# Max-unpooling on one core: the first image made in eight VectorE instructions on half images instead of four on whole ones

## The chip, the cores and the metric

The kernel runs on one core of one Trainium2 chip. The metric is the device time of one execution in microseconds (us), and the tables give the median of several executions. "Span" is the time from the first to the last instruction in the profiled execution. It is about 1.3 us shorter than the device time of the same execution (71.54 us against a span of 70.2 us before the change).

## The reference

Each input element goes to one of four places in its own 2x2 output block. The other three places get zero.

```python
batch, channels, h, w = 16, 64, 32, 32          # x float32, indices 0..3, kernel_size 2
output = np.zeros((batch, channels, 2 * h, 2 * w), dtype=np.float32)
# for every b, c, i, j:
idx = indices[b, c, i, j]
output[b, c, 2 * i + idx // 2, 2 * j + idx % 2] = x[b, c, i, j]
```

The indices arrive as 64-bit integers, so 4.19 MB of x and 8.39 MB of indices are read and 16.78 MB are written.

## The kernel before

The 1024 images (batch times channels) lie on 128 partitions, T = 8 images on each. They are made in four groups of G = 2. All loads are issued before anything else, from one queue, in the order: indices of image 0, indices of images 1 and 2, all of x, the other indices. VectorE waits for all of x and then makes each image with four instructions, one for each place in the 2x2 block: (index == place) * x, written with stride 2.

```python
nc.vector.wait_ge(x_in, 16).then_inc(x_in, -16)          # all of x
for t in range(T):
    g, k = t // G, t % G
    if t in (0, FIRST):                                  # FIRST = 3
        ...                                              # wait for the indices' first or second part
    if k == 1 and t != FIRST and g:
        continue                                         # image already made together with its neighbour
    n = 1 if k == 1 or t + 1 == FIRST or not g else 2    # images in one instruction
    if g == NG - 1:
        nc.vector.wait_ge(stored_0, 16).then_inc(stored_0, -16)   # group 3 reuses group 0's buffer
    ...
    for pidx in range(4):
        op = nc.vector.scalar_tensor_tensor(
            out=o_c[:, k : k + n, :, pidx // 2, :, pidx % 2],
            in0=idx_c[:, t : t + n], scalar=pidx, in1=x_c[:, t : t + n],
            op0=mybir.AluOpType.is_equal, op1=mybir.AluOpType.mult)
    if k + n == G:
        op.then_inc(made, 1)                             # group complete

for g in range(NG):                                      # the queue that also issued the loads
    nc.sync.wait_ge(made, g + 1)
    nc.sync.dma_start(out=out_v[g], in_=out_t[g]).then_inc(stored if g else stored_0, 16)
```

## Time and profile before

| | before |
|---|---|
| device time, median of 3 (range) | 71.61 us (71.50 to 71.64) |
| span of the profiled execution | 70.2 us |
| VectorE (DVE in the profile) busy | 35.9 us, 24 instructions, 19.5 to 55.4 us |
| DMA engines, share of the span with a packet | 97.6% |
| first store: issued, first packet | 28.70 us, 30.64 us |

The transfers, as the page lists them (what is moved, issuing queue, count, KB each, median us from issue to landing; the two small loads of indices are left out):

```profile
out_dram<-out_t SPq DMA_DIRECT2D x4, 4096.0 KB, 13.5
idx_t<-in_indices_dram SPq DMA_DIRECT2D x1, 5120.0 KB, 30.1
x_t<-in_x_dram SPq DMA_DIRECT2D x1, 4096.0 KB, 18.4
```

The large load of indices takes 30.1 us to land because it stands last in the queue, behind the other loads, and not because it is slow: its own packets run only from 18.5 to 31.1 us. The other views of this profile are read in the prediction.

### The profile page before, as it was taken

To read this page: it belongs to the slowest core of one execution; us is meant where nothing else is said; L and a number is where in the kernel's file an instruction comes from. 1 tells how busy PE (TensorE), PEld (TensorE's weight loads), DVE (VectorE), ACT (ScalarE), POOL (GpSimd) and SP (SyncE) were. 2 spreads that over 40 slices of the span, in tenths; PEclk is the share of its full clock that TensorE was granted. 3 is DMA by queue.
4 is the path that set the end of the run, shared out by engine and by line. 5 is a ranking of instruction groups with operands and counts; after the bars stand their busy time and mean duration, and the time that the engine had idled before them with its cause. 6 is when DMAs were issued, how large, how long until landed. Compare 5 with 4: busy or idle time off the path is not lost.

```text
span 70.2 us, 77 instructions
## 1 busy us (share of the span) xinstructions
DVE 35.9 (51%) x24; POOL 0.2 (0%) x4
## 2 busy tenths in 40 slices
DVE  0000000000089999999999999999999500000000
POOL 1000000000000000000000000000000000000000
DMA  4999996969988899869799796969798896969790
GB/s 84 397 425 439 448 597 299 597 299 523 448 373 373 373 653 467 373 299 560 336 485 411 317 579 299 597 299 579 317 541 355 373 523 299 597 299 579 317 579 19
DMA packets 1152, 29.36 MB, mean 418 GB/s; under 512 B 128, under 2 KB 128, under 8 KB 128
## 3 DMA queue, kind: packets, MB, share of 16 engines
q1 hardware_dynamic: 1152, 29.36, 97.6%
HBM read 12.58 MB, written 16.78 MB: 418 GB/s over the span
## 4 chain that ended last, share of the span: by engine, by line
DVE 46%; DVEq 4%; issue 1%
DVE out_t L140 46%; DVEq L190 4%
## 5 line engine op out<-in xcount | busy, mean ns | idle before, releaser
L140 DVE SCALAR_TENSOR_TENSOR out_t<-idx_t,x_t 128x1024 f32<-128x1024 int32 (+1 forms) x24 | 35.9, 1572 | 19.5 <-DVEq L128 19.5
L176 POOL MEMSET const-bfloat16-1.0<- 128x1 bf16 x1 | 0.1, 101 | 0.0
L176 POOL MEMSET const-uint8-127<- 128x1 uint8 x1 | 0.1, 101 | 0.0
L176 POOL MEMSET const-float32-0.0<- 128x1 f32 x1 | 0.1, 98 | 0.2 <-issue 0.2
L176 POOL MEMSET const-float32-1.0<- 128x1 f32 x1 | 0.1, 98 | 0.0
## 6 DMA issues: line engine op xcount, KB each, us to landing
out_dram<-out_t SPq DMA_DIRECT2D x4, 4096.0 KB, 13.5
idx_t<-in_indices_dram SPq DMA_DIRECT2D x1, 5120.0 KB, 30.1
x_t<-in_x_dram SPq DMA_DIRECT2D x1, 4096.0 KB, 18.4
idx_t<-in_indices_dram SPq DMA_DIRECT2D x1, 2048.0 KB, 9.1
idx_t<-in_indices_dram SPq DMA_DIRECT2D x1, 1024.0 KB, 4.7
```

What stands on the lines that cost most here:

```text
L140: op = nc.vector.scalar_tensor_tensor(out=o_c[:, k : k + n, :, pidx // 2, :, pidx % 2], in0=idx_c[:, t : t + n], scalar=pidx, in1=x_c[:, t ...
L176: nc = _bacc.Bacc("TRN2", target_bir_lowering=False, num_devices=1)
L190: with _tile.TileContext(nc) as tc:
```

## The change

The apparent intent is to give VectorE smaller first pieces. Only image 0 is affected: its rows are cut in two, and the four instructions run once for each half. No load, wait or store moves.

```diff
-            for pidx in range(4):
-                op = nc.vector.scalar_tensor_tensor(
-                    out=o_c[:, k : k + n, :, pidx // 2, :, pidx % 2],
-                    in0=idx_c[:, t : t + n],
-                    scalar=pidx,
-                    in1=x_c[:, t : t + n],
+            parts = (slice(0, H // 2), slice(H // 2, H)) if t == 0 else (slice(0, H),)
+            for rows in parts:
+                for pidx in range(4):
+                    op = nc.vector.scalar_tensor_tensor(
+                        out=o_c[:, k : k + n, rows, pidx // 2, :, pidx % 2],
+                        in0=idx_c[:, t : t + n, rows],
+                        scalar=pidx,
+                        in1=x_c[:, t : t + n, rows],
...
```

More of the change, by code (lines that the diff above doesn't have):

```diff
@@ L138 @@
             )
-            for pidx in range(4):
-                op = nc.vector.scalar_tensor_tensor(
-                    out=o_c[:, k : k + n, :, pidx // 2, :, pidx % 2],
-                    in0=idx_c[:, t : t + n],
-                    scalar=pidx,
-                    in1=x_c[:, t : t + n],
-                    op0=mybir.AluOpType.is_equal,
-                    op1=mybir.AluOpType.mult,
-                )
+            parts = (slice(0, H // 2), slice(H // 2, H)) if t == 0 else (slice(0, H),)
[6 more added lines that the diff above has]
+                        in1=x_c[:, t : t + n, rows],
+                        op0=mybir.AluOpType.is_equal,
+                        op1=mybir.AluOpType.mult,
+                    )
             if k + n == G:
```

## The prediction

> **What bounds the kernel now.** I read the page's rows by engine and by slice first, then the DMA queue row, then the groups of instructions with shapes kept apart, the timeline around the stores, the queue's own waits, the busy time by stretches, and last the chain that ended last. The chain comes last because here it can mislead.
>
> The page: the slices of VectorE and of the DMA engines, and the queue row (packets, megabytes, share of the 16 engines' time).
>
> ```profile
> DVE  0000000000089999999999999999999500000000
> ...
> DMA  4999996969988899869799796969798896969790
> ...
> q1 hardware_dynamic: 1152, 29.36, 97.6%
> ```
>
> VectorE works only in the middle 36 us of the 70.2 us span. The DMA engines hold a packet for 97.6% of the span. The dips to 6 and 7 in the row are no pauses: a packet here lasts up to 1.5 us against a slice of 1.76 us, and a whole packet seems to be counted in the slice in which it starts. In longer stretches (columns: stretch, length, VectorE busy, GpSimd busy, clock, DMA share, GB/s) the share is level:
>
> ```profile
> 1.00:12.00 11.00, 0.00 (x0) 0.00 (x0) 1.00 1.04 429
> 12.00:30.00 18.00, 10.49 (x10) 0.00 (x0) 1.00 1.01 437
> 30.00:42.00 12.00, 12.00 (x9) 0.00 (x0) 1.00 1.01 434
> 42.00:55.40 13.40, 13.37 (x7) 0.00 (x0) 1.00 1.00 433
> ```
>
> Loads give way to stores around 31 us, and no stretch drops. From the trace's packet records I laid out every packet by start and duration: from 1.6 us on, 16 packets are in flight at every moment until 69.4 us. On each engine the first packet of the first store starts 6 ns after the last load's closing packet has begun; the first such start is at 30.64 us, the last at 31.11. A 32 KB packet takes 1.213 us, so 16 engines move 16 x 32768 B / 1.213 us = 432 GB/s, and 29.36 MB need 67.9 us. Add 1.0 us before the first packet, about 0.6 us of ragged start, and 0.4 us after the last packet, and the 70.2 us is accounted for. **The kernel is bound by bytes through the DMA engines**, and the only question about any VectorE change is whether a store comes to the queue too late.
>
> The groups, and where the stores are issued:
>
> ```profile
> L140 DVE SCALAR_TENSOR_TENSOR out_t<-idx_t,x_t 128x1024 f32<-128x1024 int32 x16 | 18.3, 1217 | 19.5 <-DVEq L128 19.5
> L140 DVE SCALAR_TENSOR_TENSOR out_t<-idx_t,x_t 128x2048 f32<-128x2048 int32 x8 | 17.7, 2282 | 0.0
> ...
> 19.50 35.87 DVE L140 SCALAR_TENSOR_TENSOR out_t<-idx_t,x_t 128x1024 f32<-128x1024 int32 x24 [19.50 <-DVEq L128]
> 28.70 27.03 SPq L153 DMA_DIRECT2D out_dram<-out_t  x4
> ```
>
> VectorE starts at 19.50 us, when x has landed, and then never idles (35.87 us busy of 35.87). The first store is issued at 28.70 us, once images 0 and 1 are done. Eight instructions lie between, so from start to start one on 1024 elements takes about (28.69 - 19.50) / 8 = 1.135 us with the overlap taken out, which the trace's start times confirm (1135 ns).
>
> The chain and the queue's own waits:
>
> ```profile
> 19.50 12.00 DVE out_t L140 x11
> ...
> 44.36 11.01 DVE out_t L140 x5
> ...
> SPq L153 <- DVE out_t L140: 51.9, 4, 26.3
> ```
>
> Both seem to say that VectorE holds the stores back. They only say that the sequencer that issues stores waits for VectorE. While it waits, the DMA engines still work through what was issued before. The chain ends with VectorE at 55.37 us; the remaining 15 us are transfers.
>
> [...]
>
> **The change part by part.** It *removes* four instructions on 1024 elements (image 0) and *adds* eight on 512. Elements, results and order of images are the same, and no wait moves: image 0 still starts only when both inputs are there, the one increment that releases the first store is still on the last instruction of image 1, and the loads and stores are the same descriptors. The built program confirms it: VectorE goes from 24 to 28 such instructions, and the queue's rows are unchanged.
> - Old image 0: 4 x 1135 = 4540 ns from start to start.
> - New image 0: [...]8 x 601 = 4808 ns. Their profiled duration should be about 1217 - 512 x (2282 - 1217)/1024 = 685 ns, so busy time as summed by the group rises more, unless overlap is merged.
> - Difference: four more fixed parts, 4 x 68 = **0.27 us** on VectorE. All later VectorE work shifts by it: the end from 55.37 to 55.64 us, store issues from 28.70 to 28.97 us for the first and from 55.4 to 55.7 us for the last.
>
> What lies on the path to the end? The first load needed 1.0 us from issue to first packet. With that, the first store could start at 28.97 + 1.0 = 29.97 us, while its engines are busy with loads until 30.64 us: 0.66 us of slack remain of 0.93. Later stores have more: the last is issued at 55.7 us and ready at 56.7, while store 2 occupies the engines until 59.7, 3 us of slack. The fourth group reuses the first group's buffer and waits for the first store, landed by 41.5 us; VectorE gets there only at 46.6, so that wait stays empty. Sum on the path: 0.27 us of extra work, 0 us of it seen. I expect 71.6 us, the time of before.
>
> **The rivals.** *One: the first store is late and VectorE's cost shows in full.* This holds if the latency of an issue under a loaded queue is not 1.0 us but near the 1.94 us seen between issue (28.70) and first packet (30.64). For it: the trace only bounds that latency from above for a busy queue. Against it: the 6 ns gap between last load and first store looks like a queue already full, not one just in time. It would make 71.6 + 0.27 = 71.9 us. *Two: a half image costs its whole duration instead of its start-to-start time.* Then 8 x 685 - 4540 = 0.94 us are added, the first store is ready at 30.64 us, just as the first engine comes free; the time is 71.6 to 71.7, and with both rivals together about 72.5 (+1.3%). Against it: start-to-start has been below duration for every neighbour in the trace. *Three: finer pieces speed something up*, by letting the first store go sooner. Against it: the store needs all of images 0 and 1, and no load is cut to match the halves. Even a VectorE of zero cost would find the engines busy with loads until 30.64. It would make 71.6, at best some hundredths less.
>
> **Range and chances.** The three times of before span 71.50 to 71.64. Below, nothing in the change removes a byte, so 71.4 covers scatter only. Above, 71.9 covers rival one in full. To pass 2% the time must move by 1.43 us, which no rival reaches: slower 0.01, faster 0.01, within 2% 0.98.
>
> **What would show it.** Right: a group of eight on 128x512 with a mean near 685 ns; VectorE's work ending near 55.6 us; the first store issued near 29.0 us but its first packets still starting near 30.6 us behind the loads; the queue share near 97.6%; span near 70.2. Wrong: a stretch around 30 to 32 us in which engines hold no packet (rival one), a first issue near 29.6 us (rival two), or a first packet earlier than the end of the loads (rival three). A start delay of the first load or a lower transfer rate would also move the time, but the change does not touch either.

The forecast's sum: 8 x 601 = 4808 ns for the new image 0 against 4540 for the old, 0.27 us more on VectorE, 0 us of it on the path to the end, 71.6 us. The 601 ns and the fixed part of 68 follow from the start times of this trace: an instruction on 1024 elements takes 1135 ns from start to start, one on 2048 takes 2202. So 1024 elements more cost 1067 ns, 68 ns of the 1135 remain as fixed, and 512 elements should cost 1067 / 2 + 68 = 601 ns. For the order of the transfers the argument had the packet records, where the first store starts 6 ns after the packet that closes the loads has begun.

## The result, and the profile after

The changed kernel takes 71.66 us (6 executions, 71.43 to 71.76) against 71.65 us for the kernel before (6 executions, 71.50 to 71.67). The ratio is 0.9997 with a 95% interval of 0.9979 to 1.0016: the same. A ratio here and below is the mean time of one kernel's runs divided by that of the other's in the same rounds, so it is not quite the ratio of the medians quoted.

The page of the changed kernel, slices and queue row:

```profile
DVE  0000000000089999999999999999999700000000
...
DMA  4999996979988999869898998979698989989790
...
q1 hardware_dynamic: 1152, 29.36, 97.4%
```

VectorE reaches a little further into its last slice (7 in place of 5). The DMA row is as full as before, with the same 1152 packets.

The groups of instructions of the changed kernel, shapes kept apart (count, then busy us and mean ns of one):

```profile
L143 DVE SCALAR_TENSOR_TENSOR out_t<-idx_t,x_t 128x2048 f32<-128x2048 int32 x8 | 17.7, 2282 | 0.0
L143 DVE SCALAR_TENSOR_TENSOR out_t<-idx_t,x_t 128x1024 f32<-128x1024 int32 x12 | 13.7, 1218 | 0.0
L143 DVE SCALAR_TENSOR_TENSOR out_t<-idx_t,x_t 128x512 f32<-128x512 int32 x8 | 4.9, 686 | 19.6 <-DVEq L128 19.6
```

The eight half images are the third row. Their 686 ns overlap: from start to start the trace has 602 ns, and image 0 takes 4.82 us in place of 4.55.

The timeline of the changed kernel (start, length in us):

```profile
19.64 36.15 DVE L143 SCALAR_TENSOR_TENSOR out_t<-idx_t,x_t 128x512 f32<-128x512 int32 x28 [19.64 <-DVEq L128]
29.12 27.03 SPq L156 DMA_DIRECT2D out_dram<-out_t  x4
```

VectorE runs for 36.15 us in place of 35.87, a difference of 0.28 us. It started 0.14 us later in this execution, because the last packet of x ended 0.14 us later (19.00 us in place of 18.86). Both together put the first store's issue at 29.12 us, 0.42 us later than before.

Busy time by stretches, first the kernel before and then the changed one (stretch, length, VectorE, GpSimd, clock, DMA share, GB/s):

```profile
26.00:30.60 4.60, 4.60 (x5) 0.00 (x0) 1.00 0.99 427
30.60:34.00 3.40, 3.40 (x4) 0.00 (x0) 1.00 1.07 463
```

```profile
26.00:30.60 4.60, 4.60 (x5) 0.00 (x0) 1.00 1.00 433
30.60:34.00 3.40, 3.40 (x4) 0.00 (x0) 1.00 1.03 443
```

The second row of each is where a late store would show. The share can exceed 1 because the view counts a whole packet in the stretch in which it starts. The trace also keeps a record of every packet, with its start, duration and size but without its engine; the packets of one engine are found as those that follow one another within a few ns. In these packet records the first store's packets start at 30.52 us, directly behind the loads, as they did before at 30.64.

The chain that ended last, of the changed kernel:

```profile
19.64 11.93 DVE out_t L143 x15
...
44.78 11.01 DVE out_t L143 x5
```

The queue's own waits, of the changed kernel (total us, times, longest):

```profile
SPq L156 <- DVE out_t L143: 52.3, 4, 26.7
```

Both look just as alarming as before and mean as little: the sequencer waits for VectorE a little longer, 52.3 us in place of 51.9, and the time does not move.

### The profile page after: what moved, and what is told of

The parts are those of the page before. It is cut to its first block, busy times and chain, and to the rows that moved or that the text cites. A ratio compares the mean times of both kernels' runs of the same rounds, so it can differ in the third digit from the quotient of the medians.

```text
span 70.3 us, 81 instructions
## 1 busy us (share of the span) xinstructions
DVE 36.1 (51%) x28; POOL 0.2 (0%) x4
## 2 busy tenths in 40 slices
DMA packets 1152, 29.36 MB, mean 417 GB/s; under 512 B 128, under 2 KB 128, under 8 KB 128
## 3 DMA queue, kind: packets, MB, share of 16 engines
q1 hardware_dynamic: 1152, 29.36, 97.4%
## 4 chain that ended last, share of the span: by engine, by line
DVE 45%; DVEq 5%; issue 2%
DVE out_t L143 45%; DVEq L193 5%
## 5 line engine op out<-in xcount | busy, mean ns | idle before, releaser
L143 DVE SCALAR_TENSOR_TENSOR out_t<-idx_t,x_t 128x1024 f32<-128x1024 int32 (+2 forms) x28 | 36.1, 1370 | 19.6 <-DVEq L128 19.6
```

The source lines that it names most:

```text
L143: op = nc.vector.scalar_tensor_tensor(out=o_c[:, k : k + n, rows, pidx // 2, :, pidx % 2], in0=idx_c[:, t : t + n, rows], scalar=pidx, in1 ...
```

## The experiments

Three theories are in play. **Hidden**: a store needs some latency from issue to first packet, then waits until the loads leave the engines, and VectorE's extra time vanishes in that wait. **No slack**: the same, but with a latency so long that nothing is hidden. **VectorE on the path**: the chain of waits taken at its word. The runs were made in three calls, each on another chip, and every ratio compares kernels within one call. The kernel before had a median of 71.61 us in the first, 71.56 in the second and 71.60 in the third. At the bar of 2% only first_8, first_16 and early_x_first_8 count as slower; smaller differences are read below where the interval leaves out 1.

| run | VectorE instructions | first store issued, us | median us | ratio (95%) |
|---|---|---|---|---|
| first_4 | 36 | 29.90 | 71.52 | 0.9997 (0.9981 to 1.0013) |
| first_8 | 52 | 30.88 | 73.45 | 1.0256 (1.0242 to 1.0270) |
| first_16 | 84 | 32.93 | 74.61 | 1.0418 (1.0405 to 1.0432) |
| merged | 20 | 28.52 | 71.60 | 1.0000 (0.9987 to 1.0014) |
| repeat_first_2 | 26 | 31.15 | 72.74 | 1.0168 (1.0154 to 1.0182) |
| repeat_last_1 | 25 | 28.80 | 71.53 | 0.9997 (0.9984 to 1.0011) |
| early_x | 24 | 22.93 | 72.77 | 1.0166 (1.0151 to 1.0182) |
| early_x_first_8 | 52 | 24.83 | 73.17 | 1.0228 (1.0214 to 1.0243) |
| split_x_wait_all | 24 | 28.79 | 71.62 | 1.0001 (0.9985 to 1.0016) |
| early_x_repeat_3 | 27 | 26.17 | 72.85 | 1.0171 (1.0154 to 1.0188) |
| last_4 | 52 | 28.97 | 72.04 | 1.0066 (1.0050 to 1.0082) |
| last_3 | 44 | 28.71 | 71.83 | 1.0031 (1.0017 to 1.0045) |

All twelve gave correct results.

### Finer and finer: first_4, first_8, first_16

The change is carried on to quarters, eighths and sixteenths of image 0.

```diff
-            parts = (slice(0, H // 2), slice(H // 2, H)) if t == 0 else (slice(0, H),)
+            cuts = 4 if t == 0 else 1        # 8 and 16 in the other two
+            parts = [slice(q * H // cuts, (q + 1) * H // cuts) for q in range(cuts)]
```

> Image 0 in quarters: 16 instructions on 256 elements in place of 4 on 1024. With the fixed part of 68 ns measured from start to start, VectorE is delayed by 12 x 68 = 0.82 us against the kernel before and issues the first store at about 29.5 us of the span. Theory 'hidden' (a store takes about 1.0 us from issue to its first packet, as the first load did, and then waits until the loads leave the engines at 30.5 to 30.6 us): just at the edge, 71.65 us, no idle engines around 31 us. Rival 'no slack' (an issue beside a busy queue takes up to the 1.4 us that the changed kernel showed): the first packet comes at 30.9 us, about 0.3 us of idle engines, 71.9 us. Rival 'VectorE on the path' (the chain of waits taken at its word): the 0.82 us show in full, 72.5 us.

> Image 0 in eighths: 32 instructions on 128 elements. VectorE is delayed by 28 x 68 = 1.90 us against the kernel before, first store issued at about 30.6 us. 'Hidden with 1.0 us latency': first store packet at 31.6 us in place of 30.6, so about 1.0 us of idle engines and 72.6 us: half of the delay is paid. 'No slack' with 1.4 us latency: first packet at 32.0, 73.0 us. 'VectorE on the path': 1.90 us in full, 73.55 us.

> Image 0 in sixteenths: 64 instructions on 64 elements. VectorE is delayed by 60 x 68 = 4.08 us if the fixed part does not grow for such short instructions; first store issued at about 32.8 us. 'Hidden with 1.0 us latency': the first store is now the late one, its packets start at 33.8 us, 3.1 us of idle engines, 74.8 us. 'VectorE on the path': 4.08 us in full, 75.7 us. In both the step from eighths to sixteenths is paid in full, 2.2 us; a smaller step would say that something else takes over.

The rows of the pieces, one fence for each kernel:

```profile
L146 DVE SCALAR_TENSOR_TENSOR out_t<-idx_t,x_t 128x256 f32<-128x256 int32 x16 | 5.5, 418 | 19.9 <-DVEq L128 19.9
```

```profile
L146 DVE SCALAR_TENSOR_TENSOR out_t<-idx_t,x_t 128x128 f32<-128x128 int32 x32 | 6.6, 283 | 19.8 <-DVEq L128 19.8
```

```profile
L146 DVE SCALAR_TENSOR_TENSOR out_t<-idx_t,x_t 128x64 f32<-128x64 int32 x64 | 8.8, 216 | 19.6 <-DVEq L128 19.6
```

From start to start the trace has 336, 202 and 135.5 ns. Subtract the 1067 ns that 1024 elements add between 1024 (1135 ns) and 2048 (2202 ns), in proportion (267, 133 and 67 ns), and 69 ns remain in all three. The two large sizes themselves give 68, and the half images (602 ns) 69, so one straight line fits every size that was run.

The stretch behind the loads, for quarters, eighths and sixteenths:

```profile
30.60:34.00 3.40, 3.40 (x4) 0.00 (x0) 1.00 1.08 463
```

```profile
30.60:34.00 3.40, 3.40 (x4) 0.00 (x0) 1.00 0.73 308
```

```profile
30.60:34.00 3.40, 3.40 (x5) 0.00 (x0) 1.00 0.36 154
```

With quarters the engines stay full. With eighths and sixteenths a hole opens, 0.96 and 2.98 us deep as a mean over the 16 engines in the packet records. From issue to first store packet the records show 0.86, 0.84 and 0.85 us in the three kernels, counted from the start of the issuing instruction, which itself takes 0.33 to 0.35 us (the four stores of the kernel before). That settles the latency for this kernel: a store must be issued by about 30.63 - 0.85 = 29.8 us, and what comes later is paid. Quarters, issued at 29.90 us, stand at this edge, with a hole of 0.03 us. They cost nothing measurable although VectorE does 0.82 us more than before. Sixteenths cost 3.00 us of their 4.08, as "hidden" had it.

Eighths do not fit. "Hidden" gave 72.6 us and the runs have 73.45, close to the 73.55 of "VectorE on the path". The page of that kernel has a row that the kernel before does not have:

```profile
q1 hardware_dynamic: 1152, 29.36, 95.4%
q14 instruction: 1, 0.01, 0.0%
```

An instruction packet of 8 KB passed through one DMA engine at 63.74 us, while the last stores ran. It took 0.31 us, and the store packets before and after it took 1.50 and 1.57 us in place of 1.21. That engine ended at 71.67 us and the others between 70.68 and 70.85. In the kernel before, the last store was issued at 55.40 us and landed 14.8 us later, at 70.2 us, 0.3 us after the slowest engine had ended at 69.84. If the end follows the slowest engine, it moved by 71.67 - 69.84 = 1.83 us, which is the measured 1.84. Whose instructions the packet carries, and what triggers it 6.2 us after VectorE's last instruction (57.56 us), the runs do not show. With sixteenths the instruction packet came at 27.8 us, in the loads. It made the latest engine end its loads at 31.77 us, but the first store's packets start only at 33.77, so the hole absorbed the delay.

This also explains a miss of the expectation for sixteenths. It had the step from eighths to sixteenths paid in full, 2.2 us by its figures, and said that a smaller step would mean that something else takes over. The measured step is 1.16 us. The hole did grow by 2.02 us, but the 0.82 us by which one engine ended after the others in the eighths is gone.

### The change turned round: merged

```diff
-            if k == 1 and t != FIRST and g:
+            if k == 1 and t != FIRST:
                 continue
-            n = 1 if k == 1 or t + 1 == FIRST or not g else 2
+            n = 1 if k == 1 or t + 1 == FIRST else 2
```

> The change turned round: images 0 and 1 together in four instructions on 2048 elements in place of eight on 1024. VectorE ends 4 x 68 = 0.27 us earlier than in the kernel before, first store issued at about 28.4 us. 'Hidden': the first store packet stays at 30.5 to 30.6 us, 71.65 us, same. 'VectorE on the path': 71.38 us.

It measured 71.60 us: four instructions fewer give nothing, just as four more cost nothing. Its timeline:

```profile
28.52 27.03 SPq L153 DMA_DIRECT2D out_dram<-out_t  x4
```

The first store was issued at 28.52 us, and its first packet still started at 30.70.

### More delay with fewer instructions: repeat_first_2

Two extra instructions on image 0 write to a spare tile, so that the delay comes without a long program.

```diff
+            for r in range(2 if t == 0 else 0):
+                nc.vector.scalar_tensor_tensor(
+                    out=spare[:, r : r + n], in0=idx_c[:, t : t + n], scalar=r,
+                    in1=x_c[:, t : t + n],
+                    op0=mybir.AluOpType.is_equal, op1=mybir.AluOpType.mult)
             for pidx in range(4):
```

> The kernel before with two extra instructions on 1024 elements ahead of image 0 (into a spare tile; the result stays right). This delays VectorE by 2 x 1.135 = 2.27 us, more than the 1.90 us of image 0 in eighths, but with 26 instructions in place of 52. First store issued at about 28.7 + 2.27 = 30.97 us. Theory 'slack and fetch' (a store needs 0.85 us from issue to first packet; what comes later than the end of the loads at 30.63 to 31.1 us is paid[...]): first store packet at 31.8 us, about 1.0 to 1.2 us paid, no instruction packet during the run, 72.6 to 72.8 us, less than image 0 in eighths (73.45) although VectorE is later. Rival 'the delay is paid nearly in full once it passes about 1 us', which the eighths' +1.84 us for 1.90 us suggest: 73.8 us.

Cut from this expectation is a guess at what the 8 KB packet is; it put the rest of the eighths' cost down to that packet. The word "fetch" in this theory's name, here and below, is the same guess, which no run shows.

It measured 72.74 us. Its timeline and its stretch behind the loads:

```profile
31.15 27.03 SPq L165 DMA_DIRECT2D out_dram<-out_t  x4
```

```profile
30.60:34.00 3.40, 3.40 (x4) 0.00 (x0) 1.00 0.73 308
```

The store is issued 0.27 us later than with eighths, the hole is as deep in this view (1.20 us in the packet records), no instruction packet comes, and the kernel is 0.7 us faster than eighths. So the eighths' extra cost belongs to the longer program and not to the delay.

### Delay in the last group: repeat_last_1

```diff
+            for r in range(1 if g == NG - 1 else 0):
+                ...                          # as above, one instruction on two images
             for pidx in range(4):
```

> One extra instruction on 2048 elements (spare tile) ahead of the last group: VectorE and the issue of the last store are 2.20 us later, at about 57.6 us; first packet possible at 58.45 us, while store 2 holds the engines until 59.7 us. 'Slack': 71.6 us, same. 'VectorE on the path' as the chain that ended last reads: 73.8 us.

It measured 71.53 us. Its timeline:

```profile
28.80 29.23 SPq L165 DMA_DIRECT2D out_dram<-out_t  x4
46.58 2.28 DVE L143 SCALAR_TENSOR_TENSOR spare<-idx_t,x_t 128x2048 f32<-128x2048 int32 x1
```

The row of the four stores stretches from 27.03 to 29.23 us because the last is issued 2.2 us later, and nothing ends later. VectorE is not on the path even in its last group.

### An earlier start: early_x, early_x_first_8 and two controls

The load of x is cut after image 2, and VectorE waits for the second part only at image 3.

```diff
-        program.first(nc.sync.dma_start(out=x_t, in_=x_v).then_inc(x_in, 16))
+        x_cut = FIRST * N
+        for q, part in enumerate((slice(0, x_cut), slice(x_cut, T * N))):
+            program.first(nc.sync.dma_start(out=x_t[:, part], in_=x_v[:, part]).then_inc(x_in[q], 16))
...
-        nc.vector.wait_ge(x_in, 16).then_inc(x_in, -16)
...
             if t in (0, FIRST):
                 half = int(t == FIRST)
+                nc.vector.wait_ge(x_in[half], 16).then_inc(x_in[half], -16)
```

> The kernel before with the load of x cut after image 2, so that images 0 to 2 can start at about 12.5 us instead of 19.5. 'Bound by bytes': VectorE issues the first store near 22 us, its first packet still starts only behind the loads at 30.6 us, 71.6 us, same. A theory in which the start of VectorE or of the first store sets the end: several us faster.

The second kernel has image 0 in eighths besides.

> The same early x, with image 0 in eighths as before (52 VectorE instructions). VectorE has some 8 us of slack, so the 1.9 us of extra VectorE work can not reach a store. 'Slack' without any cost of the instruction count: 71.6 us. 'Slack and fetch': an 8 KB instruction packet still comes during the stores, holds one DMA engine for 0.9 us and makes the last store that much later: 72.5 us, with one engine ending about 0.9 us after the rest. 'Paid in full' (1.9 us): 73.5 us.

My expectation for early_x was a miss: 72.77 us, 1.2 us slower than the kernel before. Its timeline and the stretch around the change from loads to stores:

```profile
22.93 32.53 SPq L159 DMA_DIRECT2D out_dram<-out_t  x4
```

```profile
27.40:32.50 5.10, 0.04 (x1) 0.00 (x0) 1.00 1.05 360
```

The first store is issued 5.8 us earlier, as planned. Its packets still wait for the loads, but now the last load packets are slow: each takes 2.3 to 2.8 us in place of 1.51. The loads end about 1.2 us later, and everything after them moves along. Two controls followed. The first keeps the cut of x and waits for both parts before image 0:

```diff
+        for s in x_in:
+            nc.vector.wait_ge(s, 16).then_inc(s, -16)
         for t in range(T):
...
-                nc.vector.wait_ge(x_in[half], 16).then_inc(x_in[half], -16)
```

> Control for early x, which came out 1.2 us slower than the kernel before against my expectation: the last load packet of every engine took about 2.5 us there instead of 1.51. The load of x is cut in the same way, but VectorE waits for both parts before image 0, so the first store is issued near 28.7 us again. Theory 'a store that stands in the queue well before the loads end slows their last packets': 71.6 us, last load packets at 1.51 us. Theory 'the cut of the load of x costs it': 72.8 us.

It measured 71.62 us, with the last load packets at 1.51 us again. The same stretch in it:

```profile
27.40:32.50 5.10, 5.10 (x6) 0.00 (x0) 1.00 1.07 463
```

So the cut of x costs nothing. (463 - 360) GB/s over 5.1 us is 0.53 MB, which at the 432 GB/s of the prediction is 1.2 us: the whole loss of early_x. The second control is early_x with three spare instructions in front, written as in repeat_first_2, with `range(3 if t == 0 else 0)`:

> Early x with three extra instructions on 1024 elements (spare tile) ahead of image 0: first store issued near 22.9 + 3.4 = 26.3 us, [...]before the last load packets start (29.1 to 29.4 us). Theory 'a store that stands in the queue before the last load packet starts slows it': 72.8 us, as in early x. Theory 'it takes many us in the queue, or VectorE idling in the middle': nearer 71.6 us.

It measured 72.85 us, with last load packets of 2.4 to 2.7 us, although its first store came 3.2 us later than in early_x and VectorE worked until 30.7 us. The same stretch in it:

```profile
27.40:32.50 5.10, 3.28 (x3) 0.00 (x0) 1.00 1.05 353
```

So an idle VectorE is not the reason. What is left is that the first store stands in the queue before the last load packets start, at 29.1 to 29.4 us. One rival remains in these three kernels: they all start VectorE early as well, at 13.6 to 13.7 us, and no run starts it early and issues the store late. The kernels that start VectorE near 19.5 us speak against this rival, because the stall begins in them too. With an issue between 28.52 and 28.80 us the store could be at the engines 0.85 us later (an estimate from the late stores), at 29.37 to 29.65 us, while the last load packets run (29.12 to 31.11 us in the kernel before). In four of these five kernels some of the 16 packets are then slower, up to 1.76 us in merged, 1.68 in the kernel before and 1.77 in last_3, which is too little to show in the time. With an issue at 29.90 us or later all 16 take 1.51 us. How the waiting store slows the loads in front of it, these runs do not show.

early_x_first_8 measured 73.17 us. It shares the stall, so its comparison is early_x: 0.40 us more, for which the expectation had 0.9. An instruction packet came at 59.83 us, and its engine ended at 71.39 us, against 71.15 for the next and 71.09 for the slowest engine of early_x. That accounts for 0.30 of the 0.40 us; the rest stays open. The 1.9 us of VectorE work did not show, since that would have made 74.7.

### A longer program without any delay that matters: last_4 and last_3

The kernel before with the last group in quarters, then in thirds, of single images.

```diff
+            cuts = 4 if g == NG - 1 else 1   # 3 in last_3
+            ims = [(k + m, t + m, 1) for m in range(n)] if cuts > 1 else [(k, t, n)]
+            for ko, ti, m in ims:
+                for q in range(cuts):
+                    rows = slice(q * H // cuts, (q + 1) * H // cuts)
+                    for pidx in range(4):
+                        ...                  # image ti, m images, these rows only
```

> The last group (images 6 and 7) in 32 instructions on 256 elements in place of 4 on 2048: 52 VectorE instructions, as in image 0 in eighths, and 28 x 68 = 1.9 us more VectorE work, but where the last store has about 3.4 us to spare (one extra instruction of 2.2 us there cost nothing). 'Slack and fetch': an 8 KB instruction packet comes during the stores, one engine ends about 0.9 us late, 72.2 to 72.5 us. 'Instruction count costs nothing by itself': 71.6 us. 'VectorE on the path': 73.5 us.

> The same with the last group in 24 instructions on 320 or 352 elements: 44 VectorE instructions, 1.4 us more VectorE work, hidden as well. It only places the count at which the instruction packet appears: 36 had none, 52 had one. Without it 71.6 us, with it 72.2 to 72.5 us; I lean to none.

last_4 measured 72.04 us, 0.44 more than the kernel before and less than the 72.2 to 72.5 expected. Its queue rows:

```profile
q1 hardware_dynamic: 1152, 29.36, 96.8%
q14 instruction: 1, 0.01, 0.0%
```

The instruction packet came at 63.68 us, and its engine ended at 70.44 us against 69.94 for the next. That is 0.49 us, about the loss in the median; the profiled execution was the slowest of the five (72.26 us). The cause was as expected and the size was not. The hit engine lost 0.70 us here (0.31 for the packet and 0.39 on the store packet behind it, where first_8 had 0.95 in all), and about as much as sticks out beyond the next engine (0.49 us) is lost in the time (0.44 us).

last_3 measured 71.83 us, 0.2 us more than before and outside the scatter. This lies between its two expectations. Its profile shows no instruction packet and an unchanged span of 70.2 us. In all four executions the device time is about 1.6 us longer than the span, in place of 1.3, so those 0.2 us lie outside the span. What they are stays open.

## Why the prediction was right

- **The bound.** Right. The kernel is limited by bytes through the DMA engines, which have a packet for 97.6% of the span before and 97.4% after, and VectorE's 0.28 us more shows nowhere. repeat_last_1 and merged moved VectorE by +2.2 and -0.27 us without moving the time.
- **The cost of the cut.** Right: 0.27 us predicted, and image 0 took 0.27 us longer. The mean of 685 ns measured 686, the start-to-start time of 601 ns measured 602, and the fixed part of 68 ns came back as 69 at four sizes.
- **The slack.** The mechanism was right and its latency mis-sized: 1.0 us was taken from the first load, and late stores show 0.84 to 0.86. The changed kernel's first store, issued at 29.12 us, was therefore ready at 29.97 us, 0.54 us before its engines came free. The mis-sizing was on the safe side and changed nothing. The predicted issue at 28.97 us missed by 0.15 us, because VectorE started 0.14 us later in that execution.
- **Rival one**, a latency near 1.9 us, is refuted by the changed kernel, whose first packet came 1.40 us after the issue, and by first_4, which would have cost the whole of its 0.82 us.
- **Rival two**, half images at their full duration, is refuted by the start-to-start times.
- **Rival three** was rightly rejected for this change, but part of the reason given was wrong. The prediction said that even a VectorE of zero cost would find the engines busy with loads until 30.64 us, and would make 71.6 us, "at best some hundredths less". In early_x a store that was ready early made the loads end at 31.70 to 32.36 us and the time 72.77. The change itself does not go there, since it makes the first store later. For a change that speeds VectorE up by 2.5 us or more the argument would probably have failed, by my estimate: from 28.70 us it would move the issue of the store to 26.2 us, where early_x_repeat_3 (26.17 us) had the stall. No run made VectorE itself that fast.
- **The sums.** Three are loose, and none bears on the result. (28.69 - 19.50) / 8 is 1.149 us and not 1.135; the start times do give 1.135. The parts of the span add up to 69.9 us and not 70.2; they leave out the ragged end, where engines finish between 69.36 and 69.84 us. The longest packet of the kernel before lasts 1.68 us and not 1.5.
- **Not foreseen**: that adding instructions can cost time apart from their work. At 28 instructions it did not happen. At 52 it did: all three kernels of that count show an instruction packet and an engine that ends late, each in the one execution that was profiled. The packet appeared with 52 and 84 VectorE instructions and not with 44 or fewer.

## What to carry to other kernels

When the DMA engines are full from start to end (here a packet on them for 97.6% of the span), ask of a compute change only when its transfers reach the queue: here a store had to be issued before 29.8 us, and cutting image 0 in two kept to that, and in four just about. The chain that ended last named VectorE in the fast and in the slow kernels alike (45.9% of the span before, 49.0% with eighths), so read the packets around the change from loads to stores instead. Do not assume that earlier is safe or that instructions are free: in early_x and early_x_repeat_3 a first store issued at 22.93 and 26.17 us in place of 28.70 cost about 1.2 us, and in last_4 28 extra instructions came with an instruction packet and 0.4 us in a place where their work was hidden.
